# A raw key/value weight tile lands in a context key buffer, and two pieces of VectorE work change places in the opening of a two-layer diffusion backbone

## The chip, the core and the metric

The kernel runs on one core of a Trainium2 chip. The core has four engines that compute, each with an instruction queue of its own: TensorE (PE in the profile; its weight loads are PEld), VectorE (DVE), ScalarE (ACT) and GpSimd (POOL). SyncE (SP) issues most of the DMA transfers. The metric is the device time of one execution in microseconds: 1722.77 us as the median of three runs (1722.7 to 1722.93).

## What is computed

Two layers over 512 latent tokens of width 1024, beside a prefix of 256 context tokens that use the same weights. Layer 0 is windowed attention with 16 query heads of width 64 and 4 key/value heads, layer 1 a bidirectional retention; each is followed by a gated feed-forward block. Every norm is modulated by columns (shift, scale, gate) that come from a conditioning vector. Cut to the parts that the opening works on:

```python
mx = jnp.split(c_act @ ada_w[i] + ada_b[i], 6, axis=-1)       # columns for the latent tokens
mc = jnp.split(cc_act @ ada_w[i] + ada_b[i], 6, axis=-1)      # columns for the context
h_x = modulate(rms_norm(x, norm1_g[i]), mx[0], mx[1])
h_c = modulate(rms_norm(y_ctx, norm1_g[i]), mc[0], mc[1])
...
q_x, k_x, v_x = jnp.split(h_x @ w_qkv, [qd, qd + kvd], axis=-1)
k_c, v_c = jnp.split(h_c @ w_qkv[:, qd:], 2, axis=-1)
...
log_g = jax.nn.log_sigmoid(decay_logit.astype(f32))           # layer 1's decays
```

## The kernel before

**Tiling.** Tokens lie along the free dimension and the width in eight tiles of 128 partitions, so the residual stream is eight tiles `res` of 128 x 512 for the latent tokens and half as wide ones for the context. A weight tile is 128 x 1024 floats (512 KB). Each matrix product of full precision is made of three: a weight is split into a high part `whi` (a cast on ScalarE) and a low part `wlo` (the difference, on VectorE), the hidden state `h` into two parts as well, and high x high, low x high and high x low are added up in PSUM.

**The opening** is everything up to the attention, some 70 us. It does four things that interleave:

- the sums of squares of both streams (`squares0`, `rms`), from which the norms come;
- the modulation columns of layer 0. Shift and scale of the first norm come in four *quarters* (`ada_quarter_load`, `ada_quarter`), each of four tiles of 512 KB; four *units* of four more tiles (`unit_load`, `ada_unit`; `UNITS`) hold the later columns. The products of a quarter (L345) and of a unit (L315) give rows, which ScalarE copies (L348, L318), TensorE transposes (L352, L322) and VectorE adds to a bias (L358, L359, L114; L325);
- the hidden states `h` (latent) and `hc` (context): `hidden0`, with VectorE's L438 and L443 and ScalarE's cast L439;
- the key and value products (`keys`, L450; `values`, L464) with four weights: raw tiles loaded by `load_w` (L377), high parts by `split_w` (L382), low parts by `split_low` (L386).

**Buffers.** The quarters, the units after the first, and the third and fourth raw key/value weights all use the tag `adan` of the pool `st`: eight slots of 512 KB, in rotation. A load must wait until the tile that had its slot has been read for the last time. The first unit's eight half tiles have `k` buffers of the pool `akv`, which are the latent key buffers of later; `kc` is the tag of the context keys in the same pool, first used by `key_parts` after the opening. `pT` are two PSUM banks that take the rows and the transposed columns in turn.

**What sets the order.** TensorE, VectorE and ScalarE run the opening in the order in which it is written (`manual_schedule`); what stands outside of that block, such as the table of decays for layer 1 (L802 to L819: `lg` and `dcol`, 21 instructions on VectorE with at most 8 columns and two on ScalarE), is put in by a scheduler. SyncE issues the loads in the order of the program, one after the other: if one waits, so do all behind it. Each load also waits for the load eight places before it on the same ring of semaphores (DMAHW0 to DMAHW7).

`off_grid` sets aside a few columns, so that the tiles behind it begin 64 bytes off a step of 256, and a second call brings them back on it.

Of the kernel before, what the change touches and what calls it, by code (L numbers as in the profile page):

```python
# [9 lines left out]
F32R = mybir.dt.float32r  # L10
BF16 = mybir.dt.bfloat16
AF = mybir.ActivationFunctionType
ALU = mybir.AluOpType

P = 128
# [34 lines left out]
def dit_kernel(ctx, tc, xT, cT, crow, small, consts, masks, tabs0, tabs1, jtab, adaQ, adaN, adaT, wst, out):  # L50
    nc = tc.nc
# [10 lines left out]
    def T(pool, cols, tag, bufs, dt=F32):  # L62
        return pool.tile([P, cols], dt, tag=tag, bufs=bufs, name=tag)
# [25 lines left out]
    turn = {"pre": None, "lnexp": [], "silu": []}  # L89

    def after(ins, others):
        for o in others:
            tc.add_manual_dep(ins.ins, o.ins.name, order, reason="table set turn")
# [74 lines left out]
    def load_stream(s, engines=(nc.sync, nc.sync)):  # L168
        res = []
        if s == 0:  # L170
            for k in range(KT):
                t = T(rp, 512, "res", 12)
                eng = engines[k % 2] if k < 4 else nc.sync
                ins = eng.dma_start(t, xT[:, k, :])
                if eng is nc.scalar:
                    turn["lnexp"].append(ins)
                res.append(t)
        else:
            for k in range(0, KT, 2):
                t = T(rp, 512, "res", 12)  # L180
                nc.sync.dma_start(t.rearrange("p (a n) -> p a n", a=2), cT[:, k:k + 2, :])
                res += [t[:, 0:SC], t[:, SC:2 * SC]]
        return res
# [44 lines left out]
    def off_grid(pool, cols):  # L228

        nc.gpsimd.memset(T(pool, cols, "off%d" % cols, 1), 0.0)  # L230
# [99 lines left out]
    def ada_quarter_load(q):  # L330
        w = []
        for i in range(4):
            w.append(T(st_p, 1024, "adan", 8))
            nc.sync.dma_start(w[i], adaQ[q, i // 2, i % 2])
        return w
# [31 lines left out]
    akv = AK.enter_context(tc.tile_pool(name="akv", bufs=1, reuse_waits="tile"))  # L367
# [3 lines left out]
    st_p = St.enter_context(tc.tile_pool(name="st", bufs=1, reuse_waits="tile"))  # L371
# [3 lines left out]
    def load_w(pool, tag, bufs):  # L375
        raw.append(T(pool, 1024, tag, bufs))
        nc.sync.dma_start(raw[-1], wst[wpos[0]])  # L377
        wpos[0] += 1
# [5 lines left out]
    def split_low():  # L384
        i = lows.pop(0)
        nc.vector.tensor_tensor(wkv[i][1], raw[i], wkv[i][0], op=sub)  # L386
# [7 lines left out]
    load_w(st_p, "adan", 8)  # L394
    wq.append(ada_quarter_load(1))
    res0[1] = load_stream(1)
    load_w(st_p, "adan", 8)
    wq += [ada_quarter_load(2), ada_quarter_load(3)]
    rope0 = T(akv, 1024, "rope0", 1)
    nc.sync.dma_start(rope0.rearrange("p (a n) -> p a n", a=2), tabs0)  # L400
    mask = T(akv, NM * P, "mask", 1, BF16)
# [13 lines left out]
    def busy(n):  # L415

        nc.tensor.matmul(kvv[2][:, :n], ones, res0[0][0][:, :n], start=True, stop=True)
# [5 lines left out]
    def stats0(s):  # L423
        squares0(s)
        cond_silu(ccol)
        ln_exp_turn()
        rms(s, bank=pT)
# [17 lines left out]
    def keys(s, q):  # L445
        for j in range(2):
            o = kvx[j] if s == 0 else kvc[:, j * SC:(j + 1) * SC]
            for i, (a, b) in enumerate(((0, 0), (1, 0), (0, 1))):
                for k in (2 * q, 2 * q + 1):
                    last = nc.tensor.matmul(o, wkv[j][a][:, k * P:(k + 1) * P], h[s][k][b],  # L450
                                            start=k + i == 0 and (s == 0 or j == 0),
                                            stop=k == KT - 1 and i == 2, skip_group_check=s == 1)
        return last
# [15 lines left out]
    with tc.manual_schedule(engines={mybir.EngineType.PE, mybir.EngineType.DVE, mybir.EngineType.Activation}):  # L469
        for n in (SX, SX, SX, SX, 256):  # L470
            busy(n)
        stats0(0)
        c1 = ada_quarter(0, wq[0], lambda: busy(256))
        split_w(st_p)
        busy(SX)
        hidden0(0, 0, 1, between=(split_low,))
        c1()
        split_w(st_p)
        split_low()
        keys(0, 0)  # L480
        split_w(rp)
        split_low()
        squares0(1)
        c1 = ada_quarter(1, wq[1], lambda: values(0, 0, (0, 1)))
        hidden0(0, 2, 3)
        c1()
        values(0, 0, (2, 3))
        rms(1, bank=pT)
        keys(0, 1)
        c1 = ada_quarter(2, wq[2], lambda: values(0, 1, (0, 1)))  # L490
        c1()
        hidden0(1, 0, 1)
        split_w(rp)
        hidden0(1, 2, 3)
        values(0, 1, (2, 3))
        c1 = ada_quarter(3, wq[3], lambda: (keys(1, 0), hidden0(0, 4, 5)))
        c1()
        split_low()
        keys(1, 1)
        hidden0(0, 6, 7)  # L500
        keys(0, 2)
        c1 = ada_unit(UNITS[0], wu[0])
        hidden0(1, 4, 5)
        hidden0(1, 6, 7)
        c1()
        values(1, 0)
        values(1, 1)
        c1 = ada_unit(UNITS[1], wu[1])
        for i, mt in enumerate(mtmp):
            nc.vector.tensor_copy(mask[:, 4 * i * P:4 * i * P + mt.shape[1]], mt)  # L510
        keys(1, 2)
        c1()
        c1 = ada_unit(UNITS[2], wu[2])
        keys(0, 3)
        last_key = keys(1, 3)
        c1()
        c1 = ada_unit(UNITS[3], wu[3])
# [6 lines left out]
    kx, kc = {}, {}  # L524
    kn = [T(ap, 512, "tt", TTB) for _ in range(3)]
# [19 lines left out]
        nc.vector.tensor_tensor(kn[i], kn[i], y, op=mult)  # L545

    def key_parts(e, src, tag="k", bufs=8):
        k1, k2 = T(akv, 512, tag, bufs, F32R), T(akv, 512, tag, bufs, F32R)
        src = src[64 * e:64 * e + 64, :]
        nc.scalar.copy(k1[0:64, :], src)  # L550
        nc.scalar.copy(k2[64:128, :], src)
        hi_same = (k1[0:64, :], k2[64:128, :])[e]
        nc.vector.tensor_tensor(k1[64:128, :], src, hi_same, op=sub)
        nc.vector.tensor_tensor(k2[0:64, :], src, hi_same, op=sub)
        return k1, k2
# [86 lines left out]
    with tc.manual_schedule(engines={mybir.EngineType.PE}):  # L642
        after(values(0, 2), [last_key])
        c1()
        rope_key(kn[0])
        key_factor(0)
        q0[0]()
        key_factor(1)
        for e in range(2):
            kx[e] = key_parts(e, kn[0])  # L650
        q0[1]()
        off_grid(akv, 16)
        for e in range(2):
            k1, k2 = key_parts(e, kn[1], "kc", 4)
            kc[e], kc[2 + e] = ((k1[:, c], k2[:, c]) for c in HALVES)
        off_grid(akv, 48)
        q0[2]()
        values(0, 3)
        q0[3]()
        values(1, 2)  # L660
        values(1, 3)
# [135 lines left out]
    dec = sm_t[:, C_DEC:C_DEC + 8]  # L797
    lg = cp.tile([P, 8], F32, name="lg")
    t1 = cp.tile([P, 8], F32, name="lg_t1")
    t2 = cp.tile([P, 8], F32, name="lg_t2")  # L800
    t3 = cp.tile([P, 8], F32, name="lg_t3")
    after(nc.scalar.activation(t1, dec, AF.Abs), [turn["pre"]])  # L802
    lnexp(t1, t1, AF.Exp, scale=-1.0)
    nc.vector.tensor_scalar(t2, t1, 2.0, None, op0=add)
    nc.vector.reciprocal(t2, t2)
# [560 lines left out]
    for hd in range(RH):  # L1366
# [24 lines left out]
        Y, X, kc = W4("Y"), W4("X"), W4("X")  # L1391
# [572 lines left out]
```

## Time and profile before

| | |
|---|---|
| median of three runs | 1722.77 us |
| profiled execution: time | 1725.47 us |
| profiled execution: span in the trace | 1723.7 us |
| TensorE busy, matmuls | 1697.5 us (98%) |
| VectorE busy | 1341.2 us (78%) |
| ScalarE busy | 867.9 us (50%) |
| GpSimd busy | 65.7 us (4%) |
| mean granted TensorE clock | 0.998 |
| DMA, whole span | 209.57 MB, 122 GB/s |
| DMA, first 70 us | 24.41 MB, 349 GB/s |

The page has one row for each engine, but its shares are means over all stages. The opening is a stage of its own: there the transfers run near 416 GB/s, against 122 GB/s over the whole span. So it has to be read from views that are cut to it: the chain of waits in order of time (what released each step), tables by stage, each engine's timeline, and the waits of SyncE's queue. A timeline row gives the start, the length, the engine, the line, the operation, output <- inputs, the count, and in brackets the idle time before it and what ended that.

### The profile page before, as it was taken

The numbers are of one execution on the slowest core, as the hardware profiler recorded it, in microseconds if no ns is written. First come the engines' busy times: TensorE is split into PE (matmuls) and PEld (weight loads), VectorE is DVE, ScalarE is ACT, GpSimd is POOL, SyncE is SP. The second block draws the span as 40 slices with busy tenths as digits, with TensorE's granted clock in tenths as the row PEclk, the third lists the DMA queues.
The fourth block names the chain that finished last, engine by engine and source line by source line (L and its number), as shares of the span: only waits on it lengthen the run. The fifth ranks groups of instructions, "written<-read, shape, count | busy, mean of one in ns | idle before, by whom it ended". The sixth has DMA issues, their size and how long they took to land.

```text
span 1723.7 us, 27805 instructions
## 1 busy us (share of the span) xinstructions
PE 1697.5 (98%) x10876; PEld 1514.5 (88%) x10876; DVE 1341.2 (78%) x2418; ACT 867.9 (50%) x1550; POOL 65.7 (4%) x186
## 2 busy tenths in 40 slices
PE   7999999999999999999999999999999999999999
PEld 5788877899999999999988888898898999899988
DVE  6698889788778788787879857757767898877774
ACT  5587779565433334242555534534525564445442
POOL 0000000000000000000000000000000000000000
PEclk9999999999999999999999999999999999999999
DMA  9612221633244534343443624625624323333322
GB/s 351 240 30 58 62 62 56 208 125 125 78 152 122 159 110 147 113 149 118 147 127 84 197 87 122 176 67 132 183 70 121 100 74 117 104 110 111 98 86 86
DMA packets 63378, 209.57 MB, mean 122 GB/s; under 512 B 7312, under 2 KB 8976, under 8 KB 62992
## 3 DMA queue, kind: packets, MB, share of 16 engines
q1 hardware_dynamic: 53168, 171.63, 31.1%
q0 software_dynamic: 9792, 35.66, 8.4%
q8 instruction: 85, 1.39, 0.3%
q10 hardware_dynamic: 288, 0.52, 0.1%
q14 instruction: 45, 0.37, 0.1%
HBM read 201.75 MB, written 2.10 MB: 118 GB/s over the span
## 4 chain that ended last, share of the span: by engine, by line
PE 85%; DVE 6%; DMA 6%; ACT 2%; issue 1%; SPq 0%; DVEq 0%; ACTq 0%
PE Y L897 14%; PE Z L897 7%; PE pj L147 7%; PE pj L149 7%; PE pj L148 7%; PE Z L1296 6%; PE Y L1285 3%; PE X L897 3%; DMA wraw<-in_wst_dram 3%; PE pj L1296 3%; PE pT L736 2%; PE pO L750 2%; PE S L710 2%; PE X L1285 2%; PE X L149 1%; PE X L147 1%
## 5 line engine op out<-in xcount | busy, mean ns | idle before, releaser
L164 ACT CAST whi<-wraw 128x1024 fp32r<-128x1024 f32 x264 | 276.3, 1051 | 337.8 <-PE Z L149 81.3
L165 DVE TENSOR_TENSOR wlo<-wraw,whi 128x1024 fp32r<-128x1024 f32 x264 | 321.5, 1221 | 80.2 <-ACT whi L164 78.5
L897 PE MATMUL Y<-aq,whi 128*128 128x384 f32 x640 | 173.6, 335 | 0.2 <-ACT hn L1053 0.2
L897 PEld LDWEIGHTS Y<-aq,whi 128*128 128x128 f32 x640 | 116.6, 188 | 1.7 <-ACT hn L1053 1.4
L256 DVE SCALAR_TENSOR_TENSOR res<-pj,mod,res 128x512 f32<-128x512 f32 (+1 forms) x112 | 81.1, 728 | 39.6 <-PE pj L149 39.2
L897 PE MATMUL Y<-aq,wlo 128*128 128x384 f32 x320 | 107.0, 334 | 0.0
L273 DVE CUSTOM_DVE_ANT_0 y<-adaw,crow,small_sb 128x1024 bf16<-128x1024 f32 x64 | 81.9, 1280 | 31.7 <-DMA adaw<-in_adaT_dram 31.4
L1296 PE MATMUL Z<-whi,sA 128*128 128x512 f32 x256 | 80.9, 391 | 0.0
L101 ACT ACTIVATE pr<-pr,stat,qs 128x513 f32<-128x513 f32 (+2 forms) x96 | 74.2, 774 | 9.1 <-DVE stat L717 8.8
L147 PE MATMUL pj<-ax,whi 128*128 128x512 f32 x176 | 69.2, 393 | 0.9 <-DVE res L256 0.9
L149 PE MATMUL pj<-ax,whi 128*128 128x512 f32 x176 | 68.7, 390 | 0.0
L148 PE MATMUL pj<-ax,wlo 128*128 128x512 f32 x176 | 68.6, 390 | 0.0
L147 PE MATMUL pj<-act,whi 128*128 128x512 f32 x168 | 65.6, 390 | 0.0
L148 PE MATMUL pj<-act,wlo 128*128 128x512 f32 x168 | 65.6, 390 | 0.0
L149 PE MATMUL pj<-act,whi 128*128 128x512 f32 x168 | 65.5, 391 | 0.0
L897 PEld LDWEIGHTS Y<-aq,wlo 128*128 128x128 f32 x320 | 60.1, 188 | 0.0
L711 DVE CUSTOM_DVE_ANT_0 pr<-S,mask,qs 128x256 f32<-128x256 f32 (+1 forms) x96 | 53.1, 566 | 7.9 <-PE S L710 5.4
L897 PE MATMUL Y<-sA,whi 128*128 128x256 f32 x304 | 58.1, 277 | 0.0
L1296 PEld LDWEIGHTS Z<-whi,sA 128*128 128x128 f32 x256 | 48.0, 188 | 10.4
L897 PE MATMUL Y<-hx,whi 128*128 128x256 f32 x304 | 56.3, 277 | 0.0
L736 PE MATMUL pT<-const_sb,pr 128*128 128x128 f32 x352 | 53.7, 278 | 1.2 <-ACT tt L738 0.9
L1296 PE MATMUL Z<-wlo,sA 128*128 128x512 f32 x128 | 50.4, 394 | 0.5 <-DVE wlo L165 0.5
(580 smaller groups left out, 5051.2 us busy)
## 6 DMA issues: line engine op xcount, KB each, us to landing
wraw<-in_wst_dram SPq DMA_DIRECT2D x224, 512.0 KB, 3.7
adaw<-in_adaT_dram POOLq DMA_DIRECT2D x48, 512.0 KB, 3.8
adan<-in_adaQ_dram SPq DMA_DIRECT2D x16, 512.0 KB, 9.0
wx<-in_wst_dram SPq DMA_DIRECT2D x16, 512.0 KB, 6.4
adan<-in_adaN_dram SPq DMA_DIRECT2D x12, 512.0 KB, 7.7
wx<-in_wst_dram POOLq DMA_DIRECT2D x12, 512.0 KB, 7.4
adaw<-in_adaT_dram SPq DMA_DIRECT2D x8, 512.0 KB, 4.0
wraw<-in_wst_dram POOLq DMA_DIRECT2D x8, 512.0 KB, 5.6
```

The source lines that it names most:

```text
L101: ins = nc.scalar.activation(*args, **kw)
L147: nc.tensor.matmul(o, whi, xhi, start=first, stop=False)
L148: nc.tensor.matmul(o, wlo, xhi, start=False, stop=False)
L149: return nc.tensor.matmul(o, whi, xlo, start=False, stop=last)
L164: after(nc.scalar.copy(hi, t), behind)
L165: return nc.vector.tensor_tensor(lo, t, hi, op=sub)
L256: return nc.vector.scalar_tensor_tensor(res[d], o, mods[l, s][:, part, d:d + 1], res[d], mult, add)
L273: res.append(nc.vector.tensor_tensor_reduce(junk, w, cr[:, s * 1024:(s + 1) * 1024], 1.0, sm_t[:, C_ADAB + l * 48 + j:C_ADAB + l * 48 + j ...
L736: nc.tensor.transpose(tp[:, a * P:(a + 1) * P], self.pr[(0, 2, 1, 3)[a]][:, ki * P:(ki + 1) * P], ident)
L897: nc.tensor.matmul(o, p, r, start=first and k + i == 0, stop=k == 3 and i == 2, skip_group_check=not first)
L1285: ins = nc.tensor.matmul(o[:, e * SC:(e + 1) * SC], p[:, ws], r, start=first and k + e + i == 0, stop=k == 3 and i == 2, skip_group_check= ...
L1296: ins = nc.tensor.matmul(os[t], p, r, start=first and k + i == 0, stop=k == 3 and i == 2, skip_group_check=by_k or not first)
```

## The change

```diff
@@ the loads of the opening
     wq.append(ada_quarter_load(1))
     res0[1] = load_stream(1)
-    load_w(st_p, "adan", 8)
+    off_grid(akv, 16)
+    load_w(akv, "kc", 2)
+    off_grid(akv, 48)
     wq += [ada_quarter_load(2), ada_quarter_load(3)]
     rope0 = T(akv, 1024, "rope0", 1)
@@ the written order
         hidden0(0, 0, 1, between=(split_low,))
-        c1()
         split_w(st_p)
         split_low()
+        c1()
         keys(0, 0)
@@ the masks
         for i, mt in enumerate(mtmp):
-            nc.vector.tensor_copy(mask[:, 4 * i * P:4 * i * P + mt.shape[1]], mt)
+            mask_end = nc.vector.tensor_copy(mask[:, 4 * i * P:4 * i * P + mt.shape[1]], mt)
@@ key_parts
     def key_parts(e, src, tag="k", bufs=8):
-        k1, k2 = T(akv, 512, tag, bufs, F32R), T(akv, 512, tag, bufs, F32R)
+        if tag == "kc":
+            both = T(akv, 1024, tag, bufs, F32R)
+            k1, k2 = both[:, 0:512], both[:, 512:1024]
+        else:
+            k1, k2 = T(akv, 512, tag, bufs, F32R), T(akv, 512, tag, bufs, F32R)
         src = src[64 * e:64 * e + 64, :]
@@ the context keys
-        off_grid(akv, 16)
         for e in range(2):
-            k1, k2 = key_parts(e, kn[1], "kc", 4)
+            k1, k2 = key_parts(e, kn[1], "kc", 2)
             kc[e], kc[2 + e] = ((k1[:, c], k2[:, c]) for c in HALVES)
-        off_grid(akv, 48)
@@ the table of decays
-    after(nc.scalar.activation(t1, dec, AF.Abs), [turn["pre"]])
+    after(nc.scalar.activation(t1, dec, AF.Abs), [turn["pre"], mask_end])
```

It has three parts. The raw tile of the fourth key/value weight goes into the first of two context key buffers, which are now 128 x 1024 (two keys' parts in one tile; the same bytes as four of 128 x 512 before). The second weight's low part is taken before the second column step of the first quarter. The table of decays is taken after the masks have been copied. In the pool `akv` the buffers `kc` and their two offsets now come first, and `rope0`, `mask` and `k` behind them. Lines of the changed kernel are numbered two to four higher.

**SyncE's queue**, from the context tokens' last load (L181) to the rotary table (`rope`, L400, now L402). The rows name the semaphores that each load waits for: DMAHW for the load eight places ahead, PE or DVE for the last reader of the slot. Before:

```order
19 L181 DMA res<-in_cT_dram 128x512 [waits DMAHW0_49]
20 L377 DMA adan<-in_wst_dram 128x1024 [waits DMAHW1_49,PE_49]
21 L334 DMA adan<-in_adaQ_dram 128x1024 [waits DMAHW2_49,PE_49]
22 L334 DMA adan<-in_adaQ_dram 128x1024 [waits DMAHW3_49,PE_49]
23 L334 DMA adan<-in_adaQ_dram 128x1024 [waits DMAHW4_49,DVE_49]
24 L334 DMA adan<-in_adaQ_dram 128x1024 [waits DMAHW5_49,PE_49]
25 L334 DMA adan<-in_adaQ_dram 128x1024 [waits DMAHW6_49,PE_49]
26 L334 DMA adan<-in_adaQ_dram 128x1024 [waits DMAHW7_49,PE_49]
27 L334 DMA adan<-in_adaQ_dram 128x1024 [waits DMAHW0_49,PE_49]
28 L334 DMA adan<-in_adaQ_dram 128x1024 [waits DMAHW2_49,DMAHW1_49,PE_49]
29 L400 DMA rope_175<-in_tabs_dram 128x1024
```

Now:

```order
19 L181 DMA res<-in_cT_dram 128x512 [waits DMAHW0_49]
20 L377 DMA kc<-in_wst_dram 128x1024 [waits DMAHW1_49]
21 L334 DMA adan<-in_adaQ_dram 128x1024 [waits DMAHW2_49,PE_49]
22 L334 DMA adan<-in_adaQ_dram 128x1024 [waits DMAHW3_49,PE_49]
23 L334 DMA adan<-in_adaQ_dram 128x1024 [waits DMAHW4_49,PE_49]
24 L334 DMA adan<-in_adaQ_dram 128x1024 [waits DMAHW5_49,PE_49]
25 L334 DMA adan<-in_adaQ_dram 128x1024 [waits DMAHW6_49,DVE_49]
26 L334 DMA adan<-in_adaQ_dram 128x1024 [waits DMAHW7_49,PE_49]
27 L334 DMA adan<-in_adaQ_dram 128x1024 [waits DMAHW0_49,PE_49]
28 L334 DMA adan<-in_adaQ_dram 128x1024 [waits DMAHW1_49,PE_49]
29 L402 DMA rope_179<-in_tabs_dram 128x1024 [waits DMAHW2_49]
```

The loads stand in the same order. The moved weight (row 20) waits for no slot any more, and quarters 2 and 3 (rows 21 to 28) have eight slots to themselves: row 28, the last load of quarter 3, took the first slot of quarter 2 before (it waits for DMAHW2, that slot's load, as well), and now takes one that quarter 1 had.

**VectorE's queue, first quarter and first two low parts** (L358, L359, L114 are a column step; L438 and L443 the hidden state; L386 low parts). Before:

```order
29 L386 TENSOR_TENSOR wlo<-wraw,whi 128x1024 [waits DMAHW6_49,Activation_49]
30 L443 SCALAR_TENSOR_TENSOR h<-hs,mod_74,h 128x512 [waits Activation_49] x2
31 L358 TENSOR_TENSOR mod_75<-pT,small_sb 128x2x2
32 L359 TENSOR_TENSOR mod_75<-pT,mod_75 128x2x2 [waits DVE_49]
33 L114 SCALAR_TENSOR_TENSOR acol_79<-mod_75,gm_85 128x2 [waits DVE_49]
34 L386 TENSOR_TENSOR wlo<-wraw,whi 128x1024 [waits DMAHW7_49,Activation_49]
```

Now:

```order
16 L386 TENSOR_TENSOR wlo<-wraw,whi 128x1024 [waits DMAHW6_49,Activation_49]
17 L445 SCALAR_TENSOR_TENSOR h<-hs,mod_74,h 128x512 [waits Activation_49] x2
18 L386 TENSOR_TENSOR wlo<-wraw,whi 128x1024 [waits DMAHW7_49,Activation_49]
19 L358 TENSOR_TENSOR mod_75<-pT,small_sb 128x2x2
20 L359 TENSOR_TENSOR mod_75<-pT,mod_75 128x2x2 [waits DVE_49]
21 L114 SCALAR_TENSOR_TENSOR acol_79<-mod_75,gm_85 128x2 [waits DVE_49]
```

The second low part stands ahead of the context's column step.

**VectorE's queue, the table of decays.** Before, its tail stood between the norm of the latent tokens (L199, L200) and the first column step:

```order
16 L813 TENSOR_SCALAR lg_t_1295<-small_sb 128x8 [waits DVE_49]
17 L199 SCALAR_TENSOR_TENSOR sq<-pT,sq 128x512 [waits Activation_49]
18 L814 SCALAR_TENSOR_TENSOR lg<-lg_t_1297,lg_t_1295 128x8 [waits DVE_49]
19 L200 SCALAR_TENSOR_TENSOR y_237<-sq,y_237 128x512 [waits DVE_49]
20 L816 TENSOR_SCALAR dcol<-lg 128x4 [waits DVE_49]
21 L817 TENSOR_SCALAR dcol<-lg 128x4
22 L818 TENSOR_SCALAR dcol<-lg 128x4
23 L819 TENSOR_SCALAR dcol<-lg 128x4
24 L358 TENSOR_TENSOR mod_74<-pT,small_sb 128x2x2 [waits PE_49]
```

Now it follows the masks (L512) and stands ahead of the second unit's columns (the second pair of L325, row 83):

```order
68 L512 CAST mask<-hn 128x512 [waits DMAHW3_49]
69 L512 CAST mask<-hn 128x384 [waits DMAHW4_49]
70 L808 TENSOR_SCALAR lg_t_1294<-lg_t_1293 128x8 [waits Activation_49]
71 L809 RECIPROCAL lg_t_1294<-lg_t_1294 128x8 [waits DVE_49]
72 L810 TENSOR_TENSOR lg_t_1293<-lg_t_1293,lg_t_1294 128x8 [waits DVE_49]
...
81 L822 TENSOR_SCALAR dcol<-lg 128x4
82 L823 TENSOR_SCALAR dcol<-lg 128x4
83 L325 TENSOR_TENSOR mod_74<-pT,small_sb 128x4 [waits PE_49]
```

All 21 instructions moved. TensorE's queue holds the same instructions in the same order as before.

## The prediction

> **What bounds the kernel now.** First the page, for the whole span: TensorE is busy nearly all of it, so a time won in the opening is kept only if TensorE itself gets on earlier.
>
> ```profile
> span 1723.7 us, 27805 instructions
> PE 1697.5 (98%) x10876; PEld 1514.5 (88%) x10876; DVE 1341.2 (78%) x2418; ACT 867.9 (50%) x1550; POOL 65.7 (4%) x186
> ```
>
> Then the chain of waits, read in order of time over the first 73 us (start, length, work).
>
> ```profile
> 15.30 9.36 DMA res<-in_cT_dram
> 24.68 0.42 ACT y L210
> ...
> 35.24 0.62 PE pT L345 x16
> ...
> 35.88 0.33 SPq L334
> ...
> 50.97 9.98 DMA adan<-in_adaN_dram
> ...
> 60.99 0.65 PE pT L315 x16
> ```
>
> The opening is paced by transfers. At 24.68 it waits for the context tokens. At 35.24 TensorE reads the first tile of ada quarter 2; only then, at 35.88, does SyncE issue the last tile of quarter 3, and everything behind it on that queue comes late: the first unit's tiles `k`, then the tiles `adan` of the next units, the last of which TensorE takes at 60.99. The table of stages shows the hole (length, busy times by engine, granted clock, DMA share, GB/s), and the waits of SyncE its cause.
>
> ```profile
> 25.00:35.00 10.00, 9.14 (x106) 7.25 (x104) 7.53 (x19) 5.68 (x14) 0.00 (x0) 1.00 1.03 416
> 35.00:38.00 3.00, 3.00 (x74) 2.63 (x73) 0.00 (x0) 0.37 (x1) 0.00 (x0) 1.00 0.46 137
> 38.00:42.00 4.00, 4.00 (x84) 3.87 (x83) 2.67 (x11) 1.55 (x3) 0.00 (x0) 1.00 0.88 287
> 42.00:46.00 4.00, 3.85 (x40) 3.33 (x30) 3.69 (x8) 2.86 (x6) 0.00 (x0) 1.00 1.01 373
> 46.00:61.00 15.00, 13.39 (x227) 10.76 (x227) 9.59 (x26) 3.73 (x8) 0.00 (x0) 1.00 1.03 414
> ...
> SPq L334 <- PE pT L345: 6.2, 3, 5.2
> ```
>
> The transfers run at 416 GB/s up to 35, at 137 and 287 in the seven microseconds after, and are full again from 42. The longest single wait of L334 for TensorE is 5.2 us. What this costs TensorE stands in its own timeline, the unit products of L315:
>
> ```profile
> 48.59 1.53 PE L315 MATMUL pT<-k,ccol 128*32 128x128 f32 x48
> ...
> 50.94 0.43 PE L315 MATMUL pT<-k,ccol 128*32 128x128 f32 x8 [0.18 <-DMA k<-in_adaN_dram]
> 54.89 1.96 PE L315 MATMUL pT<-adan,ccol 128*32 128x128 f32 x64
> 58.49 1.08 PE L315 MATMUL pT<-adan,ccol 128*32 128x128 f32 x32
> 59.77 0.65 PE L315 MATMUL pT<-adan,ccol 128*32 128x128 f32 x16 [0.19 <-DMA adan<-in_adaN_dram]
> 60.99 0.65 PE L315 MATMUL pT<-adan,ccol 128*32 128x128 f32 x16 [0.58 <-DMA adan<-in_adaN_dram]
> ```
>
> A unit whose tiles are there takes 1.96 us (the second, at 54.89). The first is held up at its end, the third in the middle.
>
> **The change, part by part. The buffer.** The raw tile of the fourth key/value weight leaves the eight `adan` slots for a `kc` tile. So one slot more goes round: in the new order the last load of quarter 3 waits for a slot of quarter 1, not of quarter 2, and for the load eight before it, the moved weight itself. From the timelines of SyncE and TensorE:
>
> ```profile
> 20.34 0.33 SPq L377 DMA_DIRECT2D adan<-in_wst_dram  x1
> ...
> 25.22 1.96 PE L345 MATMUL pT<-adan,ccol 128*32 128x128 f32 x64
> ...
> adan<-in_wst_dram SPq DMA_DIRECT2D x2, 512.0 KB, 9.3
> ```
>
> Quarter 1 has been read by 25.22 + 1.96 = 27.18. The moved weight is issued at 20.34 and takes about 9.3 us, so it has landed near 29.6. The last load can go out then, 6.2 us ahead of 35.88, while seven transfers are still outstanding: the hole has no cause left. What it holds, against 416 GB/s: 3 us x (416 - 137) = 837 KB, or 2.0 us, in 35 to 38; 4 x (416 - 287) = 516 KB, or 1.2 us, in 38 to 42; 4 x (416 - 373) = 172 KB, or 0.4 us, in 42 to 46. The last of these has a DMA share of 1.01, so it belongs to the small `k` tiles and stays. The stream behind the hole therefore comes between 2.0 and 3.6 us earlier; I take 3.2.
>
> TensorE cannot use all of that. **First unit:** it starts at 48.59 as before, since the work ahead of it hangs on the context tokens of 24.68, whose load was issued before anything that the change touches. It ends at 48.59 + 1.96 = 50.55 instead of 50.94 + 0.43 = 51.37. Its result is copied by ScalarE and then transposed:
>
> ```profile
> 49.37 1.38 ACT L439 ACTIVATE h<-hs,mod 128x512 fp32r<-128x512 f32 x2 [3.55 <-DVE hs L438]
> 51.48 0.27 ACT L318 COPY sq<-pT 128x128 f32<-128x128 f32 x1 [0.73 <-PE pT L315]
> ```
>
> ScalarE is free at 49.37 + 1.38 = 50.75, so the copy goes 0.73 us earlier than 51.48, and so does all that TensorE does from the transposition on up to the third unit: its list of waits has no other there. **Third unit:** it starts at 58.49 - 0.73 = 57.76 and takes 1.96 instead of 60.99 + 0.65 - 58.49 = 3.15, a further 1.19. Its last 16 products begin at 57.76 + 1.47 = 59.23. Their tile, which is there at 60.95 now, must come at least 1.7 us earlier; even the smallest shift of 2.0 gives that. Sum: 0.73 + 1.19 = 1.92 us. The fourth unit's loads wait for the second unit's slots, now at 54.16; four tiles of 0.52 MB at 414 GB/s are 5.1 us, and TensorE wants them at 66.08 - 1.92 = 64.2 or later. Among the long pieces of the chain no transfer stands between 61 and 140, only engines that wait for each other; a shift that comes through there is kept.
>
> **The VectorE moves.** The table of decays is 21 small instructions on VectorE and two on ScalarE; the second weight's low part goes ahead of three column instructions.
>
> ```profile
> 16.77 0.69 DVE L200 SCALAR_TENSOR_TENSOR y<-sq,y 128x512 f32<-128x512 f32 x1
> ...
> 17.67 0.15 DVE L358 TENSOR_TENSOR mod<-pT,small_sb 128x4 f32<-128x4 f32 x1
> ...
> 22.04 0.15 DVE L358 TENSOR_TENSOR mod<-pT,small_sb 128x4 f32<-128x4 f32 x1
> ...
> 22.50 1.23 DVE L386 TENSOR_TENSOR wlo<-wraw,whi 128x1024 fp32r<-128x1024 f32 x1
> ...
> 25.43 0.42 DVE L213 TENSOR_TENSOR y<-y,sc 128x256 f32<-128x256 f32 x1 [0.57 <-ACT sc L212]
> ```
>
> Without the table the columns of 17.67 can follow the end of L200 at 17.46: 0.21 us. The low part goes from 22.50 to 22.04: 0.46 us. Both end before the context tokens land, and VectorE idles 0.57 us before 25.43 already: I count nothing, and 0.67 as the bound if that cover fails. In its new place the table stands behind the masks:
>
> ```profile
> 12.92 0.17 DVE L804 TENSOR_SCALAR lg_t<-lg_t 128x8 f32<-128x8 f32 x1 [0.18 <-ACT lg_t L101]
> 15.98 0.17 DVE L813 TENSOR_SCALAR lg_t<-small_sb 128x8 f32<-128x8 f32 x1
> ...
> 55.31 0.69 DVE L510 CAST mask<-hn 128x512 bf16<-128x512 f32 x2
> 58.60 0.23 DVE L325 TENSOR_TENSOR mod<-pT,small_sb 128x4 f32<-128x4 f32 x2 [2.60 <-PE pT L322]
> 66.18 0.23 DVE L325 TENSOR_TENSOR mod<-pT,small_sb 128x4 f32<-128x4 f32 x2 [7.35 <-PE pT L322]
> ```
>
> From 12.92 to 16.15 are 3.2 us, with the last five some 3.8: it fills 56.0 to 59.8. Behind it waits the column read of 58.60 (57.87 in the new kernel), 1.9 us late, which frees one of two `pT` banks; TensorE wants that bank for the transposition before the read of 66.18, near 64. Four microseconds of cover: nothing. Without it the price would be those 1.9.
>
> The profiled execution took 1725.47 with a span of 1723.7, 2.70 above the median of 1722.77. Its own sum is 1725.47 - 1.92 = 1723.55; from the median it is **1720.85 us**.
>
> **Rivals.** *Fallen or new half-clock stretches.* Two more stages:
>
> ```profile
> 18.00:21.00 3.00, 1.13 (x4) 0.52 (x4) 2.93 (x6) 1.97 (x3) 0.00 (x0) 1.00 1.03 422
> 21.00:25.00 4.00, 4.00 (x10) 2.23 (x10) 3.79 (x7) 1.62 (x3) 0.00 (x0) 0.57 1.03 409
> 256.00:260.00 4.00, 3.61 (x15) 3.15 (x16) 3.49 (x19) 3.68 (x10) 0.00 (x0) 0.57 0.01 2
> ```
>
> After three microseconds with TensorE busy for 1.13, the granted clock is 0.57 over 21 to 25, and it is so again over 256 to 260. Where such a stretch falls hangs on when TensorE was last thinly used, and the change moves that. The Trainium skill, "TensorE: Matmul & The Clock Gate", Part 1 (the HAM clock gate), says that the clock is halved after a thinly used window of some 3.4 us, and that these windows run freely; the first two rows agree with the first part, and no run here shows the second. By it the window's edges would decide between B and D. Such a stretch is worth up to 4 x 0.43 = 1.7 us. *B:* everything after 62 comes earlier, and the stretch at 256 does not come again: 1.92 + 1.7, 1719.1 us. *D:* the low part's earlier place lets TensorE run dry while it waits for the context, and a stretch lands on its work of 31 to 35: -1.92 + 1.7, 1722.5 us. Against both: the three runs lie within 0.23 us, and at 256 to 260 VectorE and ScalarE are busy for 3.5 and 3.7 of 4, so a faster TensorE would wait there.
>
> *C, the change does not do what it says:* the stream comes earlier but the hole stays elsewhere, or the third unit waits for something the trace cannot show behind the DMA wait: 0 to 0.73 us, about 1722.4. For it: the stream of 46 to 61 is full anyway. Against it: it is full because it is late.
>
> *E, slower: the key buffers' new places.* With `kc` in front, keys, masks and rotary table begin 64 + 8192 + 192 = 8448 bytes further on. The score products read them:
>
> ```profile
> L710 PE MATMUL S<-kc,q 128*128 128x256 f32 x192 | 41.4, 306 | 4.1 <-DVE qs L620 2.5 <-DVE stat L711 1.5
> L710 PE MATMUL S<-k,q 128*128 128x256 f32 x64 | 14.2, 294 | 0.4 <-DVE stat L711 0.4
> ```
>
> The trace has no tile at two places. Two kinds of key tile, one size of product, differ by 12 ns; over all 192 + 128 score products that is 3.8 us: 1722.77 - 1.92 + 3.84 = 1724.7. It decides from 6 ns a product (1.92 / 320), and makes 0.2% from 17. Below nothing a gain is as possible, but a place 8448 bytes on keeps the tiles on the same step of 256 bytes, so I take zero.
>
> **Numbers.** A (as summed) 0.58, with its own range 1719.9 to 1721.9; B 0.20; C 0.08; D 0.06; E 0.08. 0.2%, about what a measurement of this kernel can tell from no change, is 3.45 us: faster means below 1719.3, slower above 1726.2. Faster: B and 0.04 of A's lower edge, 0.24. Slower: the upper part of E, 0.05, and 0.02 for what I don't see, 0.07. The rest, 0.69, lies within. The range 1718.9 to 1722.9 takes in B, C and D and leaves out E and the end of B.
>
> **What would show it.** Right: L334's 5.2 us wait gone and 35 to 38 at about 400 GB/s; the eight `k` products and both ends of the third unit without a DMA wait, 64 in 1.96 us; L529 at 66.4 instead of 68.3; the table between 56 and 60. Wrong: a DMA wait left in the third unit (then the shift was under 1.7), a start of the first unit other than 48.59 (then the VectorE moves count), a mean of the score products off by several ns, or a later gap that widens by what the opening gained.

## The result, and the profile after

The changed kernel took 1721.02 us (median of 21 runs, 1719.31 to 1723.3), the kernel before, on the same chip, 1723.76 us (21 runs, 1722.01 to 1726.83). The ratio is 0.9984, 95% interval 0.9978 to 0.999: 2.7 us less, between 1.7 and 3.8. The forecast was 1.92 us less.

The page of the changed kernel, first line, and then its table of stages with the same columns and windows as before:

```profile
span 1718.9 us, 27799 instructions
```

```profile
35.00:38.00 3.00, 3.00 (x69) 2.80 (x58) 0.00 (x0) 0.37 (x1) 0.00 (x0) 1.00 1.04 419
38.00:42.00 4.00, 4.00 (x83) 3.67 (x82) 3.35 (x12) 2.22 (x4) 0.00 (x0) 1.00 1.03 401
42.00:46.00 4.00, 3.85 (x29) 3.40 (x28) 3.70 (x7) 2.18 (x5) 0.00 (x0) 1.00 1.06 406
```

The hole in the stream is gone: 419 GB/s where there were 137, 401 where there were 287. SyncE's list of waits (total, times, longest) says the same of its cause:

```profile
SPq L334 <- PE pT L345: 1.0, 2, 0.6
```

Its timeline shows when the first tile of a later unit goes out, in the changed kernel and, second, in the one before:

```profile
42.68 13.60 SPq L306 DMA_DIRECT2D adan<-in_adaN_dram  x11
```

```profile
46.11 9.81 SPq L306 DMA_DIRECT2D adan<-in_adaN_dram  x9
```

L334 waits for TensorE 0.6 us at most, not 5.2, and the stream stands 46.11 - 42.68 = 3.4 us earlier; 3.2 had been taken. (From the second traces of both kernels the same difference is 45.91 - 43.48 = 2.4 us, so a single pair gives it to about 1 us.) TensorE's timeline of the four units, and ScalarE's two rows of the chain's end in the opening (the square of the first keys, before and after):

```profile
47.95 1.95 PE L315 MATMUL pT<-k,ccol 128*32 128x128 f32 x64
53.44 1.95 PE L315 MATMUL pT<-adan,ccol 128*32 128x128 f32 x64
57.01 1.95 PE L315 MATMUL pT<-adan,ccol 128*32 128x128 f32 x64
63.41 1.95 PE L315 MATMUL pT<-adan,ccol 128*32 128x128 f32 x64
...
65.65 0.60 ACT L531 ACTIVATE pr<-pj 128x512 f32<-128x512 f32 x1
```

```profile
68.31 0.60 ACT L529 ACTIVATE pr<-pj 128x512 f32<-128x512 f32 x1
```

Every unit runs through in 1.95 us with no wait for a transfer. The square comes at 65.65 instead of 68.31, 2.66 us earlier. Of that, 0.27 is an earlier landing of the context tokens in this execution (24.41 against 24.68); from the landing to the square it is 41.23 against 43.64 us, 2.4 us won. The forecast had 1.92 for this stretch. The first unit's start was to stay, and came 48.59 - 47.95 = 0.64 earlier, 0.37 more than the 0.27 of the landing. What lies between is VectorE's adding up of the context's squares, eight tiles of which ScalarE squares one after the other. Before:

```profile
25.00 1.31 ACT L212 ACTIVATE sc<-res 128x256 f32<-128x256 f32 x3
26.85 2.01 ACT L212 ACTIVATE sc<-res 128x256 f32<-128x256 f32 x4 [0.54 <-DVE y L213]
...
26.39 3.07 DVE L213 TENSOR_TENSOR y<-y,sc 128x256 f32<-128x256 f32 x6 [0.53 <-ACT sc L212]
```

After:

```profile
24.74 0.74 ACT L212 ACTIVATE sc<-res 128x256 f32<-128x256 f32 x2
25.63 2.53 ACT L212 ACTIVATE sc<-res 128x256 f32<-128x256 f32 x5 [0.16 <-DVE y L213]
...
25.17 3.60 DVE L213 TENSOR_TENSOR y<-y,sc 128x256 f32<-128x256 f32 x7 [0.97 <-ACT sc L212]
```

Before, the first of seven sums starts at 25.43 and is over at 25.85, and the second starts only at 26.39. By the program it waits for the first sum, which was over, and for its own square, the second of ScalarE's L212. ScalarE's first row has three squares of 0.42 and ends at 26.31, so that square was there by 25.89. After, all seven stand in one row, 0.53 us from start to start. The profile puts the pause down to ScalarE, which had nothing more to give. The pause is 0.42 us on the path that sets the end: 0.95 - 0.53 from the first sum to the second (the expectations below have it as 0.43).

### The profile page after: what moved, and what is told of

Its sections match the earlier page's. It is cut to its first block, busy times and chain, and to the rows that moved or that the text cites. A ratio compares the mean times of both kernels' runs of the same rounds, so it can differ in the third digit from the quotient of the medians.

```text
span 1718.9 us, 27799 instructions
## 1 busy us (share of the span) xinstructions
PE 1696.4 (99%) x10876; PEld 1517.7 (88%) x10876; DVE 1342.4 (78%) x2418; ACT 868.1 (51%) x1550; POOL 66.1 (4%) x186
## 4 chain that ended last, share of the span: by engine, by line
PE 87%; DVE 7%; DMA 3%; ACT 2%; issue 1%; SPq 0%; DVEq 0%; ACTq 0%
PE Y L901 15%; PE Z L901 7%; PE pj L147 7%; PE pj L149 7%; PE pj L148 7%; PE Z L1300 6%; PE X L901 4%; PE Y L1289 3%; PE pj L1300 2%; PE pT L740 2%; PE pO L754 2%; PE S L714 2%; PE X L1289 1%; PE X L149 1%; PE X L147 1%; PE X L148 1%
## 5 line engine op out<-in xcount | busy, mean ns | idle before, releaser
L740 PEld LDWEIGHTS pT<-const_sb,pr 128*128 128x128 f32 x352 | 41.0, 144 | 12.1 <-issue 4.0
```

The lines of the kernel that those rows point to most:

```text
L740: nc.tensor.transpose(tp[:, a * P:(a + 1) * P], self.pr[(0, 2, 1, 3)[a]][:, ki * P:(ki + 1) * P], ident)
```

## The experiments

Each ratio is to runs of the kernel before on the same chip at the same time, whose median was between 1724.84 and 1725.2 us (1723.76 for the first trace of the changed kernel, whose ratio is that of the result); 0.001 of it is 1.7 us. The stages are worked out from starts of instructions in each kernel's trace, in us: the first sum of the context's squares to the second; first to last product of the first and the third unit (64 products one after another take 1.68); the context's landing to the square of the first keys.

| kernel | ratio to before (95%) | sum to sum | first unit | third unit | landing to square |
|---|---|---|---|---|---|
| before, first trace | | 0.95 | 2.50 | 2.87 | 43.64 |
| before, second trace | 1.0002 (0.9993 to 1.0011) | 0.95 | 2.84 | 2.92 | 44.29 |
| changed, first trace | 0.9984 (0.9978 to 0.999) | 0.53 | 1.68 | 1.68 | 41.23 |
| changed, second trace | 0.9983 (0.9974 to 0.9992) | 0.53 | 1.68 | 1.68 | 41.19 |
| buffer alone | 0.9987 (0.9979 to 0.9996) | 0.95 | 1.68 | 1.68 | 41.59 |
| nine slots | 0.9987 (0.9974 to 0.9999) | 0.95 | 1.68 | 1.68 | 41.67 |
| changed, seven slots | 0.9999 (0.999 to 1.0008) | 0.53 | 1.68 | 3.14 | 42.48 |
| table alone | 0.9991 (0.9983 to 1.0) | 0.53 | 2.17 | 3.01 | 42.99 |
| table alone, 21 fills | 1.0003 (0.9994 to 1.0012) | 0.95 | 2.70 | 3.28 | 44.17 |
| low part alone | 1.0002 (0.9992 to 1.0011) | 0.96 | 2.87 | 2.77 | 44.14 |
| places alone | 1.0001 (0.9993 to 1.001) | 0.95 | 2.54 | 3.11 | 45.25 |
| changed, 21 fills | 0.9987 (0.9978 to 0.9996) | 1.46 | 1.68 | 1.68 | 42.12 |
| changed, 10 fills | 0.998 (0.9971 to 0.9989) | 0.53 | 1.68 | 1.68 | 41.18 |
| changed, context first | 0.9988 (0.9979 to 0.9997) | 0.52 | 1.68 | 1.68 | 44.38 |

The last row's stretch is longer because the landing is earlier there; it is read below.

**The kernel before, once more**, with no edit:

> The kernel before, once more, to see what two executions of one program differ by. All theories: ratio 1.000. In its trace the opening (to the start of ScalarE's key square L529, 68.31 us in the first trace) within 0.3 us of the first; the wait of 5.2 us of L334 again. If the 0.43 us gap between the first two context sums on VectorE (25.85 to 26.39) is chance, it is missing or different here; if half-clock stretches fall by chance, they lie elsewhere or are of another length than at 256 to 260.

It took 1724.86 us; ratio 1.0002. Its opening of 44.29 us against 43.64 is the size of what differs between executions of one program, so what a single trace shows below 0.7 us in the opening is read from the stage it stands in, not from the sum.

**The buffer alone** (the changed kernel with the written order and the table of before):

```diff
         hidden0(0, 0, 1, between=(split_low,))
+        c1()
         split_w(st_p)
         split_low()
-        c1()
...
-    after(nc.scalar.activation(t1, dec, AF.Abs), [turn["pre"], mask_end])
+    after(nc.scalar.activation(t1, dec, AF.Abs), [turn["pre"]])
```

> The change's buffer alone; the low part and the table of decays stay where they were. Theory slot (all of the gain is the transfer hole): 1.9 us off the opening, L529 near 66.4, first unit starts at 48.6 as before, ratio 0.9989. Theory sum (the VectorE moves give 0.4 to 0.7 of the 2.7 us in the opening): the first unit starts at 48.6 here too, and only the two moves bring it to 47.95. Theory chance (the 0.64 us ahead of the first unit is no effect of the change): first unit anywhere from 47.9 to 48.6.

It took 1722.71 us, 2.2 less than before (0.7 to 3.6). Its units, from TensorE's timeline:

```profile
48.33 1.96 PE L315 MATMUL pT<-k,ccol 128*32 128x128 f32 x64
...
57.39 1.95 PE L315 MATMUL pT<-adan,ccol 128*32 128x128 f32 x64
```

Both units are whole, and landing to square is 43.64 - 41.59 = 2.05 us shorter: 0.82 at the first unit, 1.19 at the third, 0.04 between. The pause of VectorE is still there (0.95). So the buffer alone brings what the forecast summed, and nothing of the 0.42.

**The low part alone** (the kernel before, `c1()` two lines later):

```diff
-        c1()
         split_w(st_p)
         split_low()
+        c1()
```

> Only the second weight's low part goes ahead of the context's column step. Theory slot: nothing, ratio 1.000, L529 at 68.3; TensorE may start quarter 1 up to 0.5 us earlier (25.22 to about 24.7) and wait for the context sums instead. Theory sum: first unit up to 0.46 us earlier, ratio 0.9997.

1724.98 us, ratio 1.0002; neither the pause nor the units are touched. The 0.46 us by which a low part comes earlier end ahead of the context's landing, as had been said.

**The table alone** (the kernel before with the table behind the masks):

```diff
-            nc.vector.tensor_copy(mask[:, 4 * i * P:4 * i * P + mt.shape[1]], mt)
+            mask_end = nc.vector.tensor_copy(mask[:, 4 * i * P:4 * i * P + mt.shape[1]], mt)
...
-    after(nc.scalar.activation(t1, dec, AF.Abs), [turn["pre"]])
+    after(nc.scalar.activation(t1, dec, AF.Abs), [turn["pre"], mask_end])
```

> Only the table of decays moves behind the masks. Theory slot: nothing, ratio 1.000, L529 at 68.3; first key product 0.2 us earlier (19.81 to 19.6), the second unit's column read 1 to 2 us late and nobody waiting for it. Theory sum: first unit 0.2 us earlier, ratio 0.9999. If the cover of the table fails: L529 up to 1.9 us later, ratio 1.001.

1723.6 us, ratio 0.9991 with 1.0 at the edge of its interval: by the time alone it is not told from nothing. Its stage tells it: VectorE's timeline has the seven sums in one row,

```profile
24.97 3.60 DVE L213 TENSOR_TENSOR y<-y,sc 128x256 f32<-128x256 f32 x7 [0.43 <-ACT sc L212]
```

and landing to square is 0.65 us shorter than in the first trace of before, 1.30 than in the second. Against the first trace that is 0.23 more than 0.42: the first unit waits 0.33 less (2.17 for 2.50) and the third 0.14 more. The hole is still there, and the two traces of before differ by 0.34 in the first unit, so the 0.23 are not told from chance.

**The table's move with its place in the queue filled up again** (the kernel with the table alone, and 21 two-element fills at the head of VectorE's queue, over by 1.5 us):

```diff
-    nc.vector.memset(grid.tile([P, 56], F32, name="off_grid"), 0.0)
+    og = grid.tile([P, 56], F32, name="off_grid")
+    nc.vector.memset(og, 0.0)
+    for i in range(21):
+        nc.vector.memset(og[:, 2 * i:2 * i + 2], 0.0)
```

> table_only with 21 tiny memsets at the very start of VectorE's queue, where it waits for the first transfer: the path is that of table_only, the number of VectorE instructions ahead of the context sums that of the kernel before. In the kernel before, VectorE sits idle 0.43 us between the first and the second context sum (starts 0.95 apart), though its operands are there 0.6 us earlier; with the table moved the starts are 0.53 apart. Theory position (the stall hangs on where an instruction stands in the queue): 0.95 again here, ratio 1.000. Theory table (it hangs on the table's instructions or ScalarE's two): 0.53, ratio 0.9992.

The pause is back, with nothing of the table near it (VectorE's timeline; lines are numbered three higher):

```profile
24.87 0.43 DVE L216 TENSOR_TENSOR y<-y,sc 128x256 f32<-128x256 f32 x1 [0.76 <-ACT sc L215]
25.82 3.08 DVE L216 TENSOR_TENSOR y<-y,sc 128x256 f32<-128x256 f32 x6 [0.52 <-ACT sc L215]
```

and the time is that of before (ratio 1.0003). So it is neither the table's work nor its two instructions on ScalarE that makes the pause, but the number of instructions ahead of the sum, or what goes with it.

**The changed kernel with 10 and with 21 fills** (the same edit in the changed kernel, `range(10)` and `range(21)`):

> As the one with 21 fills, with 10. If the stall of 0.43 us sits at one place of VectorE's queue (between two blocks of instructions, say), it is met by another instruction: the 0.43 us stand elsewhere on VectorE, some eleven instructions further on than in the kernel before, and show in the opening only if VectorE is waited for there. If it is the number of instructions since the start that matters in a coarse way, the second sum has it again (0.95). Opening between 41.2 and 41.7 us, hole filled as before (1.68 us).

> The changed kernel with 21 two-element fills more at the head of VectorE's queue, done in the first microseconds, long before the context lands. Every later instruction of VectorE keeps its work and its order and stands as many places behind the queue's start as it did before the table was moved. If the 0.43 us ahead of the second context sum hang on the place in the queue, they come back (0.95 from the first to the second sum instead of 0.53), and the opening takes 41.65 us instead of 41.23; the filled hole stays (units 1.68 us). If they hang on what the table itself does to its neighbours (its use of VectorE between the latent norm's instructions, or its two instructions on ScalarE), they stay away: 0.53 and 41.2. Time: 0.4 us above the changed kernel by the first, the same by the second, which a ratio of 0.0002 hardly tells; the stage decides.

With 10 there is no pause, here or at another instruction of the opening: the rows read as in the changed kernel, and landing to square is 41.18. With 21 the second sum starts 1.46 us after the first, half a microsecond more than the pause explains. ScalarE's timeline says why:

```profile
25.13 0.40 ACT L215 ACTIVATE sc<-res 128x256 f32<-128x256 f32 x1
26.57 0.72 ACT L215 ACTIVATE sc<-res 128x256 f32<-128x256 f32 x2 [1.04 <-DMA res<-in_cT_dram]
```

In this execution the second transfer of context tokens came late, the square of 26.57 was ready at 26.97, and VectorE started at 27.02. A pause of 0.42 us behind the first sum's end at 25.98 would have been over by then and can't be seen. So this run doesn't show whether the pause is back; what stands is the pair of the table alone without and with 21 fills, and the count over all kernels. In the order of VectorE's queue, where the instructions that only wait for a semaphore and one branch count as well (the trace has no row for the branch and shows one less), the second sum is the 65th instruction in before and in the kernels with the buffer, the low part, the places or nine slots alone and in the one with 21 fills: in all seven traces the pause is there. It is the 44th in the changed kernel, the table alone, seven slots and the context first, and the 54th with 10 fills: in all six traces it is not.

**Nine slots** (the kernel before with one more slot and nothing else moved; the 64 bytes of `off_grid` ahead of `kc` are left out for room):

```diff
-            w.append(T(st_p, 1024, "adan", 8))
+            w.append(T(st_p, 1024, "adan", 9))
...
-        off_grid(akv, 16)
```

> The kernel before with nine slots in place of eight for the raw tiles and quarters, in the old places; to make room the context key buffers lose their offset of 64 bytes. No VectorE move. Theory slot: as buffer_only, 2.0 us less from the context tokens' landing to L529 (41.6 instead of 43.6), all 64 products of the first and third unit in 1.95 us, ratio 0.9988. If the kc buffer itself matters, it stays at 43.6.

Ratio 0.9987, both units whole, 41.67 us: the same as the buffer alone. What counts is a slot more in the rotation, not where the raw weight lands.

**The changed kernel with seven slots**, so that the last load of quarter 3 waits for a tile of quarter 2 again:

```diff
-            w.append(T(st_p, 1024, "adan", 8))
+            w.append(T(st_p, 1024, "adan", 7))
```

> The changed kernel with seven slots: the raw weight is in the kc buffer and the two VectorE moves are there, but the last load of quarter 3 waits for quarter 2 again. Theory slot: the hole is back, from the context's landing to L529 about 43.1 (43.6 less the 0.43 of the second context sum), ratio 0.9992 to 1.000. If the gain were the kc buffer or the order on VectorE, it stays at 41.2 and 0.9985.

By the time the gain is gone (ratio 0.9999, 0.999 to 1.0008); by the stages only a part of it is gone. The table of stages:

```profile
35.00:38.00 3.00, 3.00 (x74) 2.74 (x73) 0.00 (x0) 0.37 (x1) 0.00 (x0) 1.00 0.59 154
38.00:42.00 4.00, 4.00 (x84) 3.77 (x82) 2.78 (x11) 1.65 (x3) 0.00 (x0) 1.00 0.97 340
```

SyncE's list of waits:

```profile
SPq L334 <- PE pT L345: 6.5, 3, 5.9
```

The third unit in TensorE's timeline:

```profile
58.99 0.64 PE L315 MATMUL pT<-adan,ccol 128*32 128x128 f32 x16 [0.47 <-DMA adan<-in_adaN_dram]
60.20 0.64 PE L315 MATMUL pT<-adan,ccol 128*32 128x128 f32 x16 [0.57 <-DMA adan<-in_adaN_dram]
```

The hole is back with its 5.9 us wait, and the third unit is held up as before (3.14 us from first to last product), with the weight in its new place and VectorE's sums in one row. The last tile of that unit is issued late as well with seven slots, at 54.57; but its products start 1.21 us after those of the tile before it, against 1.22 in before (59.77 and 60.99), so it comes at the spacing of the stream and not later for that slot. The first unit stays whole (1.68). Expected were 43.1 us from landing to square, and 42.48 are 1.16 less than in the first trace of before, about what the first unit (0.82) and the pause (0.42) are worth. The hole is shallower than before, too, with 154 and 340 GB/s for 137 and 287. So this run brings back the loss at the third unit; for the first unit the slot is shown by the buffer alone and by nine slots.

**The places alone** (the kernel before with `kc` first in its pool and in the form of the change; a fill of 16 columns takes the place of the raw weight, which stays in `adan`):

```diff
     res0[1] = load_stream(1)
+    off_grid(akv, 16)
+    nc.gpsimd.memset(T(akv, 1024, "kc", 2)[:, 0:16], 0.0)
+    off_grid(akv, 48)
     load_w(st_p, "adan", 8)
```

> The kernel before with the context key buffers put first in their pool, so that keys, masks and rotary table lie 8448 bytes further on, as in the change; the raw weight stays in its old slot, no VectorE move. Theory slot: the hole is there, ratio 1.000, and the score products keep their means (306 and 294 ns) within what two executions differ by. Rival E (places): the means of the score products move by several ns and the ratio by 0.001 to 0.002.

Ratio 1.0001. The score products, from the groups of the page:

```profile
L715 PE MATMUL S<-kc,q 128*128 128x256 f32 x192 | 41.2, 306 | 4.1 <-DVE qs L627 2.5 <-DVE stat L716 1.5
...
L715 PE MATMUL S<-k,q 128*128 128x256 f32 x64 | 14.2, 293 | 0.4 <-DVE stat L716 0.4
```

306 and 293 ns against 306 and 294 before: the places cost nothing. (The opening of this trace is 1.6 us longer than that of before, 1.4 of it ahead of the first unit, where a half-clock stretch lasted 6.8 us in that one execution instead of 3.4. That the stretch is the cause is likely, and not shown.)

**The context's tokens first** (the changed kernel, a try at more):

```diff
-    wq.append(ada_quarter_load(1))
     res0[1] = load_stream(1)
+    wq.append(ada_quarter_load(1))
```

> The changed kernel with the context tokens' four loads ahead of quarter 1's four in SyncE's queue. Theory: the opening is paced by the context's landing at 24.41, behind which 4 x 0.52 MB of quarter 1 stood, worth some 5 us of the stream. With the tokens there early, VectorE, free at 24.2, begins the sums at 24.2 instead of 25.17, and TensorE loses the 0.56 us in which it waits at 28.48 for ScalarE's copy: the products of the context's hidden state begin at 30.2 to 30.6 instead of 31.10, all later stages 0.5 to 0.9 us earlier, time 1719.7 to 1720.5 by the first medians, ratio near 0.998. Rival: quarter 1, now last, comes late; its 64 products, at 24.34 in the changed kernel, wait for a transfer and begin at 25 or later, and the gain is 0 or a loss of up to 1 us.

Ratio 0.9988, against 0.9983 for the changed kernel in the same group: no gain. VectorE's and TensorE's timelines:

```profile
24.35 3.59 DVE L213 TENSOR_TENSOR y<-y,sc 128x256 f32<-128x256 f32 x7
...
26.98 0.64 PE L345 MATMUL pT<-adan,ccol 128*32 128x128 f32 x16 [0.42 <-DMA adan<-in_adaQ_dram]
...
48.47 1.96 PE L315 MATMUL pT<-k,ccol 128*32 128x128 f32 x64
```

The sums do start as soon as VectorE is free, 0.8 us earlier than at 25.17, but quarter 1's last tile now comes at 26.98 and TensorE waits for that instead; the first unit starts at 48.47, later than in both traces of the changed kernel (47.95 and 48.10). The rival was right: the context and quarter 1 are both needed near 24.5, and the stream brings only one of them by then.

**The changed kernel, once more**, with no edit:

> The changed kernel once more. The theory (the filled hole 2.0 us, the table's move 0.4 us) expects the same opening as in its first profile: 41.2 us from the context's landing to the context key's square, second context sum 0.53 us after the first, first and third unit 1.68 us from first to last product, and a ratio near 0.9985. The half-clock stretches are held to be chance of the execution: the second, 10.2 us long at 252.4 in the first profile of the changed kernel, may be 3.4 or 6.8 long here. Rival: the longer stretch is an effect of the change; then it is 10.2 us long again, and the score products' mean is again near 310 ns.

1722.48 us, ratio 0.9983; the opening is the same to 0.04 us. On the half-clock stretch both signs that the rival named came: 10.2 us again, and 310 ns as the mean of the score products again. Whether the change is the cause is taken up under the rivals below; first, what the stretch costs. The table of stages of the first trace of the changed kernel:

```profile
250.00:254.00 4.00, 1.75 (x6) 1.31 (x7) 3.94 (x18) 1.76 (x5) 0.00 (x0) 0.80 0.20 79
254.00:258.00 4.00, 3.82 (x18) 3.49 (x17) 2.78 (x13) 4.00 (x10) 0.00 (x0) 0.50 0.02 6
258.00:262.00 4.00, 3.48 (x16) 2.69 (x15) 2.49 (x7) 3.37 (x10) 0.71 (x4) 0.50 0.00 0
```

and of the one with 10 fills:

```profile
254.00:258.00 4.00, 3.79 (x17) 3.15 (x17) 3.10 (x17) 3.73 (x9) 0.00 (x0) 0.57 0.02 6
258.00:262.00 4.00, 3.07 (x24) 2.30 (x24) 3.09 (x12) 3.89 (x12) 0.55 (x4) 1.00 0.00 0
```

The granted clock is at half for 10.2 us in both traces of the changed kernel and for 3.4 in the one with 10 fills. What that costs is seen when the start of one and the same VectorE instruction is compared in two traces. Lead over the first trace of before, in us (the columns are times in that trace):

| | at 71 | at 256 | at 271 | at 600 | end of span |
|---|---|---|---|---|---|
| before, second trace | -0.33 | -0.22 | -0.72 | -0.58 | 0.0 |
| changed, first trace | 2.67 | 2.72 | 1.02 | 1.20 | 4.84 |
| changed, second trace | 2.53 | 2.51 | 0.79 | 0.91 | 3.08 |
| buffer alone | 2.30 | 2.34 | 2.37 | 2.48 | 3.16 |
| changed, 10 fills | 2.42 | 2.40 | 2.22 | 2.40 | 1.33 |

What the opening wins is carried to 256 whole. The first trace of before has a stretch of 3.4 us there; one of 10.2 costs 1.7 more than that (2.0 in the kernel with the low part alone), one of 6.8 (the second trace of before) 0.5 more, and another of 3.4 between 0 and 0.2. From 600 to the end the two traces of the changed kernel win a further 3.6 and 2.2, and the one with 10 fills loses 1.1: what executions differ by there is as large as the stretch, and a single trace's span tells neither.

## Why the prediction was right, point by point

**The hole and its cause: right.** It went with the slot (buffer alone, nine slots) and came back, a little shallower, when the slot was taken away (seven slots). The stream came 3.4 us earlier for 3.2 in the first pair of traces and 2.4 in the second. That 3.2 lies so near 3.4 is luck, and nothing hung on it: the forecast's sum needed 1.7.

**First unit 0.73, third unit 1.19: right.** The first unit's products end 0.82 us sooner after its start, since the eight-product pieces go through without a wait, and ScalarE's copy, which the forecast held to 0.73, goes 0.81 earlier (2.08 us after the unit's start with the buffer alone, 2.89 before). The third's end comes 1.19 sooner. Buffer alone: 2.05 from landing to square, and 2.2 us in the time.

**"Both end before the context tokens land ... I count nothing, and 0.67 as the bound if that cover fails": this step failed, inside its bound.** For the low part it held (ratio 1.0002). For the table the cover held too; the 0.21 us of its work are hidden. But the table's move is worth 0.42 us in another way: it takes 21 instructions out of VectorE's queue ahead of the context's sums, and with them the pause before the second sum. That this lies under the bound of 0.67 is luck, as the bound was worked out for another cause. The start of the first unit, which the forecast had named as the sign that the VectorE moves count, did come earlier. The idle 0.57 us before 25.43 had been read as cover; the 0.53 before 26.39, a row further down the same timeline, had not been read at all, and it was not a wait for ScalarE. With it the sum is 1.92 + 0.09 + 0.42 = 2.4, and 2.4 is what the opening of the two first traces shows; the measured 2.7 (1.7 to 3.8) holds both figures, so the time alone does not tell 1.92 from 2.4.

**The table behind the masks, "Four microseconds of cover: nothing": right.** VectorE's timeline of the changed kernel:

```profile
55.24 0.17 DVE L808 TENSOR_SCALAR lg_t<-lg_t 128x8 f32<-128x8 f32 x1
...
59.00 0.22 DVE L325 TENSOR_TENSOR mod<-pT,small_sb 128x4 f32<-128x4 f32 x2
63.52 0.23 DVE L325 TENSOR_TENSOR mod<-pT,small_sb 128x4 f32<-128x4 f32 x2 [4.30 <-PE pT L322]
```

The column read of 59.00 follows the table, late as forecast, and the next comes at 63.52 with VectorE idle 4.30 us before it.

**The rivals.** C (the hole stays elsewhere) falls with the whole units. E (the key buffers' places) falls with the places alone; the changed kernel's first two traces have longer means for the same products, but the one with 10 fills, with the same places, does not. A mean near 310 ns comes in the six traces whose half-clock stretch at 256 lasts 6.83 or 10.24 us, the second trace of before among them; in the other eight it is 305 to 307. The first row is of the changed kernel, the second of that one:

```profile
L714 PE MATMUL S<-kc,q 128*128 128x256 f32 x192 | 41.9, 310 | 3.8 <-DVE qs L626 2.5 <-DVE stat L715 1.1
```

```profile
L717 PE MATMUL S<-kc,q 128*128 128x256 f32 x192 | 41.3, 305 | 4.2 <-DVE qs L629 2.5 <-DVE stat L718 1.5
```

B and D had a stretch of half clock fall away or land on the work of 31 to 35. Neither happened. What did happen at 256 is the opposite of B: the stretch got longer, and was worth the 1.7 us that B had for it, with the other sign. That the change makes it longer is not shown, and other traces speak against it: the kernel with the low part alone has 10.24 us too, and the kernels with the buffer alone and with 10 fills, which reach 256 as early to 0.4 us, have 3.41. What the length goes with is the place in the work at which the stretch begins. Its start in each trace, moved by that trace's lead at 252 onto the times of the first trace of before, sorts all fourteen traces:

| start, in times of before | traces | length of the stretch |
|---|---|---|
| 254.32 to 254.67 | before, second; table alone with 21 fills; changed with 21 fills | 6.83 us |
| 255.13 to 255.50 | changed, first and second; low part alone | 10.24 us |
| 255.59 to 256.98 | the other eight, before's first among them | 3.41 us |

The two executions of before, one program, start at 256.59 and 254.32, so the start is not fixed by the program; the two of the changed kernel happen to lie at 255.13 and 255.19. No trace of the changed kernel itself starts elsewhere; with 21 fills it starts at 254.66 and with 10 at 256.98, and the lengths there are 6.83 and 3.41. The Trainium skill, "TensorE: Matmul & The Clock Gate", Part 1 (the HAM clock gate), has the clock decided window by window, some 3.4 us each, with windows that run freely; the lengths here, 3.41, 6.83 and 10.24 us, agree with such steps, and so does it that one program shows 3.4 in one execution and 6.8 in another.

## What to carry to other kernels

Where buffers go round, find the load that waits longest for a slot and count how many slots would let it wait for a tile that was read long ago: one more was worth 2 us here, wherever it was taken from, and none of the loads had to move. Read the idle time in front of every instruction of a row on the path, not only the first, and hold the engine named against its own timeline: a pause with its operand there is worth an edit that moves the queue. And the next thing in the stream is not free for the taking: bringing the context forward only made the quarter behind it late.

## What the hardware showed beside that

A pause of 0.42 us on VectorE between two sums whose operands are there, in every trace in which the second is the 65th instruction of its queue, waits counted in (seven of seven that can show it) and in none where it is the 44th or the 54th (six); it goes when 21 instructions ahead are taken out and comes back when 21 fills are put in. What the engine does in it no row shows, and with the 65th elsewhere in the queue no such pause was seen in the opening. The half-clock stretch at 256 lasts 3.41, 6.83 or 10.24 us, also between two executions of one program; 6.83 cost 0.5 and 10.24 cost 1.7 to 2.0 us more than 3.41. In all fourteen traces the length goes with the place in the work at which the stretch begins, and starts 0.1 and 0.5 us apart have different lengths (10.24 and 3.41 us at 255.50 and 255.59, 6.83 and 10.24 at 254.67 and 255.13).
